# The chunk chain of a delta-rule mixer: three dependent products per chunk, or one map per chunk multiplied out ahead

## The chip, the cores and the metric

One core of one Trainium2 chip runs the whole kernel. The metric is the device time of one execution in microseconds (us). Before the change it was 1698.63 us, the median of three runs (1697.1 to 1699.03).

## The reference

One layer of a streaming encoder: a modulated RMS norm, one input projection, two groups of heads side by side (eight RWKV-7 heads with a matrix state, eight attention heads with a forget bias), an output projection, and a SwiGLU feed-forward part. 1024 frames of a new stream and 64 frames that continue an old one are handled in one launch, all in fp32 accuracy. What the change touches is the RWKV-7 recurrence, written frame by frame:

```python
def step(s, inp):
    r_t, w_t, k_t, v_t, kk_t, a_t = inp
    sa = jnp.einsum('bhvk,bhk->bhv', s, -kk_t)
    s = (s * w_t[:, :, None, :]
         + sa[..., None] * (kk_t * a_t)[:, :, None, :]
         + v_t[..., None] * k_t[:, :, None, :])
    return s, jnp.einsum('bhvk,bhk->bhv', s, r_t)
```

## The kernel before

**Stages.** The kernel first forms the modulation (`pada`), then runs a mixing stage of two halves (half 0: frames 0 to 511; half 1: frames 512 to 1023 and the 64 continued ones), in which the input projection (`pmm`, L321 to L323: three fp32r products per weight tile, with high and low parts), the RWKV heads and the preparation of attention are interleaved. Then come the attention of half 0 (`psc`, `ppt`, `pav`), the attention of half 1 with the output projection (`po`), and the feed-forward part (`pf..`, `pd`). The two strings in `ORDER` set the order in which the steps of the mixing stage are written; within that, a scheduler at build time sets the order of instructions on each engine. On the chip every engine works through its own list in order, so an instruction whose data are late holds back all that stand behind it.

**The RWKV heads.** Eight heads are four pairs j; a pair fills the 128 partitions, 64 rows per head. Step A (`rwkv_a`) makes the scaled keys and receptances (`rk`, `kb`), their score matrices `At` (`pA`, L491, per head on 64 rows), and starts the inverse of a unit triangular matrix per chunk of 64 frames. Step B (`rwkv_b`) finishes the inverse with small 32x32 products (`pg`, `pw`, `pu`, L550 to L576), transposes the keys (`pkbt`, L594) and the values (`pvt`, L602), and then walks the chunks. Half 0 has 8 chunks per pair, half 1 has 9, so 4 x 8 + 4 x 9 = 68 chunks in all. Step N normalises the outputs `y`.

**The chain over the chunks.** `sv[:, c]` is a tile of 128 partitions and two heads: for head h one half of the partitions holds the state, the other half the values of the chunk. Per chunk five products are issued, of which three depend on each other:

- `pR` (L624): scores times `sv`, the right side of the triangular system; the diagonal halves are copied to `R` by VectorE (L626) and ScalarE (L627).
- `pSA` (L637): the inverse times `R`; with a minus sign it replaces the state in `sv` (VectorE L638, ScalarE L639).
- `pS` (L640): the transposed keys times `sv`; two instructions of VectorE (L644) multiply by the decay `pc` and add `sd`, the decayed old state that GpSimd formed (L631). The result is the state in `sv` of the next chunk.
- `pY` (L635 and L645): two products that add up the outputs, one with the state, one with what replaced it.

An fp32 product of the program is two MATMUL instructions on the chip, a transpose is one. PSUM tags around the change: `rb` has one buffer (transposes, small products, `pY`, and the norm of step N), `ch` two (small products, `pR`, `pSA`, `pS`), `ra` two (`pA`).

## Time and profile before

| | |
|---|---|
| time, median of three runs | 1698.63 us |
| span of the profiled execution, first to last instruction | 1691.4 us |
| that span against the median | 7.2 us shorter: what lies around the first and the last instruction |
| mean granted TensorE clock | 0.992 |
| mixing stage, from about 60 to 664 us | 604 us |
| attention of half 0, to about 763 us | 99 us |
| attention of half 1, output projection and feed-forward part | from 763 us on |

The profile lists one execution. Its own time is not listed apart from its span; the 7.2 us are taken as fixed. Engines are PE (TensorE products), PEld (TensorE weight loads), DVE (VectorE), ACT (ScalarE), POOL (GpSimd) and SP (the queue that issues DMAs). A row of the timeline gives the start in us, the duration in us, engine, line, operation, output<-inputs, shape and count. Two rows that follow each other show what an instruction really takes from PE: products are pipelined, so the distance from start to start is shorter than the duration. A row of a group gives busy time and mean ns of one, then the engine's idle time before it. A row of waits gives total us, times, and the longest.

### The profile page before, as it was taken

To read this page: it belongs to the slowest core of one execution; us is meant where nothing else is said; L and a number is where in the kernel's file an instruction comes from. 1 tells how busy PE (TensorE), PEld (TensorE's weight loads), DVE (VectorE), ACT (ScalarE), POOL (GpSimd) and SP (SyncE) were. 2 spreads that over 40 slices of the span, in tenths; PEclk is the share of its full clock that TensorE was granted. 3 is DMA by queue.
4 is the path that set the end of the run, shared out by engine and by line. 5 is a ranking of instruction groups with operands and counts; after the bars stand their busy time and mean duration, and the time that the engine had idled before them with its cause. 6 is when DMAs were issued, how large, how long until landed. Compare 5 with 4: busy or idle time off the path is not lost.

```text
span 1691.4 us, 33224 instructions
## 1 busy us (share of the span) xinstructions
PE 1642.2 (97%) x12891; PEld 1438.5 (85%) x12891; DVE 1122.1 (66%) x2561; ACT 725.6 (43%) x1524; POOL 184.7 (11%) x412
## 2 busy tenths in 40 slices
PE   6999999999999999989999999999999999999999
PEld 3776776788888888667889899999999999999998
DVE  6776676757867655886887985555555556545545
ACT  4535364653545345775776633333333333111210
POOL 2102230222121212201220000000000000000000
PEclk9999999999999999998999999999999999999999
DMA  8544447541233344466564532222222215423313
GB/s 310 163 129 132 141 136 201 175 124 33 72 85 85 81 136 115 144 203 177 156 194 153 178 121 78 77 77 77 78 77 77 77 65 178 146 87 97 97 38 125
DMA packets 133580, 207.08 MB, mean 122 GB/s; under 512 B 62126, under 2 KB 70350, under 8 KB 133422
## 3 DMA queue, kind: packets, MB, share of 16 engines
q1 hardware_dynamic: 133422, 204.95, 39.6%
q8 instruction: 102, 1.67, 0.4%
q14 instruction: 56, 0.46, 0.1%
HBM read 157.65 MB, written 47.25 MB: 121 GB/s over the span
## 4 chain that ended last, share of the span: by engine, by line
PE 85%; ACT 5%; DVE 5%; DMA 4%; issue 2%; SPq 0%; ACTq 0%; DVEq 0%
PE pd L1302 15%; PE pfe L1187 8%; PE pfc L1187 7%; PE pfa L1187 7%; PE pmm L321 5%; PE pmm L322 5%; PE pmm L323 5%; PE pfb L1187 4%; PE pbs L402 2%; PE pav L989 2%; PE ppt L967 2%; PE pA L491 2%; PE po L321 2%; PE po L322 2%; PE po L323 2%
## 5 line engine op out<-in xcount | busy, mean ns | idle before, releaser
L321 PE MATMUL pmm<-hhi,whi 128*128 128x288 f32 (+1 forms) x624 | 218.2, 350 | 2.4 <-ACT pb L344 1.4
L322 PE MATMUL pmm<-hlo,whi 128*128 128x288 f32 (+1 forms) x624 | 216.4, 347 | 0.7 <-DVE hlo L299 0.7
L323 PE MATMUL pmm<-hhi,wlo 128*128 128x288 f32 (+1 forms) x624 | 214.7, 344 | 0.6 <-DVE wlo L243 0.6
L239 ACT CAST whi<-wraw 128x1024 fp32r<-128x1024 f32 (+2 forms) x116 | 99.2, 855 | 210.0 <-PE pd L1302 163.6
L1302 PE MATMUL pd<-al,whi 128*128 128x512 f32 (+1 forms) x528 | 172.4, 326 | 0.0
L1302 PE MATMUL pd<-ah,whi 128*128 128x512 f32 (+1 forms) x528 | 172.2, 326 | 0.0
L1302 PE MATMUL pd<-ah,wlo 128*128 128x512 f32 (+1 forms) x528 | 172.2, 326 | 0.0
L1306 DVE SCALAR_TENSOR_TENSOR x1t<-pd,mod,x1t 128x512 f32<-128x512 f32 x192 | 91.2, 498 | 106.6 <-PE pd L1302 105.9
L321 PEld LDWEIGHTS pmm<-hhi,whi 128*128 128x128 f32 x624 | 118.4, 190 | 13.9 <-ACT pb L344 2.0
L322 PEld LDWEIGHTS pmm<-hlo,whi 128*128 128x128 f32 x624 | 118.2, 189 | 10.9 <-DVE hlo L299 1.4
L323 PEld LDWEIGHTS pmm<-hhi,wlo 128*128 128x128 f32 x624 | 118.1, 189 | 10.7 <-issue 1.7
L243 DVE TENSOR_TENSOR wlo<-wraw,whi 128x1024 fp32r<-128x1024 f32 (+2 forms) x108 | 104.2, 964 | 19.5 <-ACT whi L239 18.7
L1302 PEld LDWEIGHTS pd<-ah,whi 128*128 128x128 f32 x528 | 99.1, 188 | 7.1
L1302 PEld LDWEIGHTS pd<-ah,wlo 128*128 128x128 f32 x528 | 99.1, 188 | 7.1
L1302 PEld LDWEIGHTS pd<-al,whi 128*128 128x128 f32 x528 | 99.1, 188 | 6.9
L1187 PE MATMUL pfc<-hh,hS 128*128 128x256 f32 (+1 forms) x352 | 101.8, 289 | 1.1 <-ACT hh L1089 1.1
L1187 PE MATMUL pfa<-hh,whi 128*128 128x256 f32 (+1 forms) x352 | 102.1, 290 | 0.0
L1187 PE MATMUL pfc<-hh,lS 128*128 128x256 f32 (+1 forms) x352 | 101.8, 289 | 0.0
L1187 PE MATMUL pfa<-hl,whi 128*128 128x256 f32 (+1 forms) x352 | 101.6, 289 | 0.0
L1187 PE MATMUL pfa<-hh,wlo 128*128 128x256 f32 (+1 forms) x352 | 101.5, 289 | 0.0
L1187 PE MATMUL pfc<-hl,hS 128*128 128x256 f32 (+1 forms) x352 | 100.7, 286 | 0.0
L631 POOL TENSOR_SCALAR sd<-sv,pc 64x64 f32<-64x64 f32 x136 | 77.0, 566 | 181.3 <-DVE sv L644 157.7
(368 smaller groups left out, 4380.7 us busy)
## 6 DMA issues: line engine op xcount, KB each, us to landing
wraw<-in_w_in_dram SPq DMA_DIRECT2D x52, 512.0 KB
wada<-in_w_ada_dram SPq DMA_DIRECT2D x48, 512.0 KB
as<-actscr SPq DMA_DIRECT2D x22, 544.0 KB
wraw<-in_w_gate_dram SPq DMA_DIRECT2D x22, 512.0 KB
wraw<-in_w_up_dram SPq DMA_DIRECT2D x22, 512.0 KB
wraw<-in_w_down_dram SPq DMA_DIRECT2D x40, 256.0 KB
wraw<-in_w_out_dram SPq DMA_DIRECT2D x16, 512.0 KB
actscr<-sg SPq DMA_DIRECT2D x22, 288.0 KB
```

Of the source, the lines that this page charges most:

```text
L239: nc.scalar.copy(hi, src)
L243: eng.tensor_tensor(lo, src, hi.bitcast(F32), op=ALU.subtract)
L321: nc.tensor.matmul(ps[0:M, 0:n], whi[:, k, 0:M], xhi[:, k, off:off + n], start=(k == 0), stop=False)
L322: nc.tensor.matmul(ps[0:M, 0:n], whi[:, k, 0:M], xlo[:, k, off:off + n], start=False, stop=False)
L323: nc.tensor.matmul(ps[0:M, 0:n], wlo[:, k, 0:M], xhi[:, k, off:off + n], start=False, stop=(k == kt - 1))
L402: nc.tensor.matmul(ps[:, 0:n], w, x[:, off:off + n], start=True, stop=True)
L491: nc.tensor.matmul(pa[h][:, i], kb[hp, c + i], rk[hp, c + i], start=True, stop=True)
L631: nc.gpsimd.tensor_scalar(sd[hsl[h]], sv[hsl[h], c, h], pc[hsl[h], c], None, op0=ALU.mult)
L967: nc.tensor.transpose(pt[0:rows, b - b0, t * P:t * P + qn], p[0:qn, pc:pc + rows], self.ident[0:qn, 0:qn])
L1187: nc.tensor.matmul(ps, l[:, k], r[:, s, k], start=(first and k == 0 and y == 0), stop=(k == 3 and y == 2), skip_group_check=True)
L1302: nc.tensor.matmul(ps[:, 0:n], w[:, i], x[:, t:t + n], start=(i == 0 and y == 0), stop=(i == len(fs) - 1 and y == 2))
L1306: nc.vector.scalar_tensor_tensor(dst, ps[:, so - off:so - off + l], self.mod[:, 40 + o, b:b + 1], dst, op0=ALU.mult, op1=ALU.add)
```

## The change

The walk over the chunks is a linear map of (state, values). The changed kernel multiplies that map out for each chunk before the walk, four chunks ("a quad") at a time. The score matrices of the chunk are transposed (`pat`) and copied to `gT`; the inverse is applied (`pgT`) and copied back to `gT`; two products per chunk, one per head on 64 rows (`pM`), give what is subtracted from the keys and the receptances, whose state blocks hold an identity and the decayed receptances. `kb` and `rk` now lie side by side in one tile `kr`, so that one subtraction per head and quad does both. In the walk one product per chunk gives the next state (`pS`, evacuated with the decay by one instruction of VectorE and one of ScalarE), and one gives the outputs (`pY`). `pR`, `pSA`, the second `pY`, `R`, `sd` and GpSimd's two instructions per chunk are gone. The transposes of keys and values are written ahead of the small products.

```diff
@@ rwkv_a
-        rk = self.rpool.tile([P, 9, P], F32, tag="rk", name="rk")
-        kb = self.rpool.tile([P, 9, P], F32, tag="kb", name="kb")
+        kr = self.rpool.tile([P, 9, 2, P], F32, tag="kr", name="kr")
+        kb, rk = kr[:, :, 0], kr[:, :, 1]
@@ rwkv_b
+        quads = [slice(c, min(nch, c + 4)) for c in range(0, nch, 4)]
...
         for h in range(2):
             nc.gpsimd.tensor_copy(At[hs, 0:nch, 0, h], rk[hs, 0:nch, 0:64])
         nc.gpsimd.tensor_copy(rk[0:64, 0:nch, 0:64], rk[0:64, 0:nch, 64:128])
-        nc.gpsimd.memset(rk[0:64, 0:nch, 64:128], 0.0)
-        nc.gpsimd.memset(rk[64:128, 0:nch, 0:64], 0.0)
+        nc.gpsimd.tensor_copy(rk[0:64, 0:nch, 64:128], At[0:64, 0:nch, 1, 1])
+        nc.gpsimd.tensor_copy(rk[64:128, 0:nch, 0:64], At[64:128, 0:nch, 1, 0])
+
+        gT = self.rpool.tile([P, 9, P], F32, tag="gT", name="gT")
+        for q in quads:
+            pt = self.ps([P, 4, P], tag="rb", name="pat")
+            for i, c in enumerate(range(q.start, q.stop)):
+                nc.tensor.transpose(pt[:, i], At[:, c, 0], self.ident)
+            nc.scalar.copy(gT[:, q], pt[:, 0:q.stop - q.start])
+        for h in range(2):
+            hs = hsl[h]
+            nc.gpsimd.tensor_copy(At[hs, 0:nch, 0, h], kb[hs, 0:nch, hs])
+            nc.gpsimd.tensor_copy(kb[hs, 0:nch, hs], self.ident[hs, hs].unsqueeze(1).to_broadcast([64, nch, 64]))
+        for q in quads:
+            m = q.stop - q.start
+            pt = self.ps([P, 4, P], tag="rb", name="pgT")
+            for i, c in enumerate(range(q.start, q.stop)):
+                nc.tensor.matmul(pt[:, i], inv[:, c], gT[:, c], start=True, stop=True)
+            nc.scalar.copy(gT[:, q], pt[:, 0:m])
+            pm = [self.ps([P, 4, 2, 64], tag="ch", name="pM") for _ in range(2)]
+            for i, c in enumerate(range(q.start, q.stop)):
                 for h in range(2):
+                    nc.tensor.matmul(pm[h][:, i], gT[hsl[h], c], At[hsl[h], c, :, h], start=True, stop=True)
+            for h in range(2):
+                nc.vector.tensor_tensor(kr[:, q, :, hsl[h]], kr[:, q, :, hsl[h]], pm[h][:, 0:m], op=ALU.subtract)
...
-            pr = self.ps([P, 2, 64], tag="ch", name="pR")
-            nc.tensor.matmul(pr, At[:, c, 0], sv[:, c], start=True, stop=True)
...
-            nc.tensor.matmul(pa, inv[:, c], R, start=True, stop=True)
...
-            nc.tensor.matmul(pS, kbt[:, c], sv[:, c], start=True, stop=True)
...
+                ps = self.ps([P, 2, 64], tag="ch", name="pS")
+                nc.tensor.matmul(ps, kb[:, c], sv[:, c], start=True, stop=True)
+                last = c == 7 or c == nch - 1
+                s0, s1 = (S[hsl[0]], S[hsl[1]]) if last else (sv[hsl[0], c + 1, 0], sv[hsl[1], c + 1, 1])
+                nc.vector.tensor_scalar(s0, ps[hsl[0], 0], pc[hsl[0], c], None, op0=ALU.mult)
+                nc.scalar.activation(s1, ps[hsl[1], 1], AF.Copy, scale=pc[hsl[1], c])
+            py = self.ps([P, 4, 2, 64], tag="rb", name="pY")
+            for i, c in enumerate(range(q.start, q.stop)):
+                nc.tensor.matmul(py[:, i], sv[:, c], rk[:, c], start=True, stop=True)
@@ run
-            self.rpool = MP("r", (("inv0", 1), ("inv1", 1), ("pc", 2), ("rk", 2), ("kb", 2), ("At", 2), ("gt", 1), ("g1", 1),
-                                  ("sv", 2), ("R", 2), ("st", 1), ("sd", 2)))
+            self.rpool = MP("r", (("inv0", 1), ("inv1", 1), ("pc", 2), ("kr", 2), ("At", 2), ("gt", 1), ("g1", 1),
+                                  ("sv", 2), ("gT", 1), ("st", 1)))
```

What the scheduler makes of it on PE is shown at three places; numbers L.. are lines of each kernel's own file, and a row is a product of the program (two MATMULs for fp32). First, on PE, one chunk in a walk of half 1, before:

```order
L624 MATMUL pR<-sv,At 128x128
L635 MATMUL pY<-rk,sv 128x128
L323 MATMUL pmm<-hhi,wlo 128x288
L321 MATMUL pmm<-hhi,whi 128x288
L322 MATMUL pmm<-hlo,whi 128x288
L637 MATMUL pSA<-R,inv_693 128x64
L323 MATMUL pmm<-hhi,wlo 128x288
L321 MATMUL pmm<-hhi,whi 128x288
L322 MATMUL pmm<-hlo,whi 128x288
L323 MATMUL pmm<-hhi,wlo 128x288
L321 MATMUL pmm<-hhi,whi 128x288
L640 MATMUL pS<-sv,kb 128x128
```

and one chunk there after the change:

```order
L646 MATMUL pS<-sv,kr 128x128
L653 MATMUL pY<-kr,sv 128x128
L323 MATMUL pmm<-hhi,wlo 128x288
L321 MATMUL pmm<-hhi,whi 128x288
L322 MATMUL pmm<-hlo,whi 128x288
L323 MATMUL pmm<-hhi,wlo 128x288
L646 MATMUL pS<-sv,kr 128x128
L653 MATMUL pY<-kr,sv 128x128
```

Three places at which PE has to wait for an evacuation (`pR`, `pSA`, `pS`), with 3 to 6 projection products between them, became one (`pS`), with 4 to 6 between one `pS` and the next.

Second, on PE, the multiplying out for two quads of the same pair after the change (nothing stands for it before; x8 are four chunks times two heads, the heads alternating):

```order
L323 MATMUL pmm<-hhi,wlo 128x288
L628 MATMUL pM<-At,gT 128x128 x8
L623 MATMUL pgT<-gT,inv_687 128x128 x4
L321 MATMUL pmm<-hhi,whi 128x288
L322 MATMUL pmm<-hlo,whi 128x288
L323 MATMUL pmm<-hhi,wlo 128x288
L321 MATMUL pmm<-hhi,whi 128x288
L322 MATMUL pmm<-hlo,whi 128x288
L323 MATMUL pmm<-hhi,wlo 128x288
L628 MATMUL pM<-At,gT 128x128 x8
L623 MATMUL pgT<-gT,inv_687 128x128
```

Projection products stand between a product and the one that needs its copy; `pgT` of the next quad directly follows `pM` of this one.

Third, on PE, the last pair's walk in half 1 before, which stands among the products of the attention of half 0 (`psc`, `ppt`, `pav`) from its first chunk on:

```order
L624 MATMUL pR<-sv,At 128x128
L939 MATMUL psc<-k2x_8033,q2x_8031 128x512
L602 MATMUL pvt<-ident,z 64x128
L943 LDWEIGHTS identb
L943 MATMUL psc<-cmask,identb 128x128
L635 MATMUL pY<-rk,sv 128x128
L637 MATMUL pSA<-R,inv_693 128x64
L989 MATMUL pav<-pth,vsx_8029 128x256
L640 MATMUL pS<-sv,kb 128x128
L645 MATMUL pY<-At,sv 128x128
L967 MATMUL ppt<-ident,p 128x128 x3
L989 MATMUL pav<-ptl,vsx_8029 128x256
```

and after, where the first product of attention comes after the walk's fifth `pS`, the first row here:

```order
L646 MATMUL pS<-sv,kr 128x128
L653 MATMUL pY<-kr,sv 128x128
L846 MATMUL pkv<-ident,fv 128x128
L942 MATMUL psc<-k1x_7653,qsx_7651 128x256
L944 MATMUL psc<-k2x_7654,q2x_7652 128x256
L948 LDWEIGHTS identb
L948 MATMUL psc<-cmask,identb 128x128
L646 MATMUL pS<-sv,kr 128x128
L653 MATMUL pY<-kr,sv 128x128
```

The last pair's small products, its multiplying out and five of its nine chunks now stand ahead of the attention, among the projection's products; four chunks stay in it.

## The prediction

> **What bounds the kernel now.** I read the page first, then the busy time by stage, then the stage of the change row by row.

> ```profile
> span 1691.4 us, 33224 instructions
> PE 1642.2 (97%) x12891; PEld 1438.5 (85%) x12891; DVE 1122.1 (66%) x2561; ACT 725.6 (43%) x1524; POOL 184.7 (11%) x412
> PE 85%; ACT 5%; DVE 5%; DMA 4%; issue 2%; SPq 0%; ACTq 0%; DVEq 0%
> ```

> The span is 1691.4 us and the median 1698.63, so 7.2 us lie around the span; they stay. PE is busy 97% of the span and makes 85% of the chain that ended last. So a stage gets shorter by what PE has to do less, or wait less, in it. The windows of the two stages in which the heads' walks run (core, then busy time and count of PE, PEld, DVE, ACT, POOL, the granted clock, DMA):

> ```profile
> 60.00:664.00 604.00, 589.87 (x5278) 473.11 (x5278) 418.47 (x1141) 295.06 (x660) 128.98 (x262) 1.00 0.41 116
> 664.00:763.00 99.00, 87.79 (x641) 67.25 (x634) 77.98 (x232) 70.39 (x204) 19.20 (x61) 0.97 0.58 172
> ```

> In the mixing stage PE idles 14 of 604 us, and no other engine is above 70%. In the attention of half 0 PE idles 11 of 99 us and DVE is at 79%. Seven of the eight walks lie in the first, the last one in the second.

> **What a chunk costs PE now.** Durations overlap, so I count from start to start. These are all the groups of PE in one walk of nine chunks, from its first `pR` to its end:

> ```profile
> L323 PE MATMUL pmm<-hhi,wlo 128*128 128x288 f32 x45 | 14.3, 319 | 0.0
> L321 PE MATMUL pmm<-hhi,whi 128*128 128x288 f32 x44 | 14.0, 319 | 0.0
> L322 PE MATMUL pmm<-hlo,whi 128*128 128x288 f32 x44 | 13.5, 308 | 0.0
> L624 PE MATMUL pR<-sv,At 128*128 128x128 f32 x18 | 3.9, 299 | 0.3 <-ACT sv L605 0.2
> L637 PE MATMUL pSA<-R,inv 128*128 128x64 f32 x18 | 3.7, 290 | 0.3 <-ACT R L627 0.2
> L640 PE MATMUL pS<-sv,kb 128*128 128x128 f32 x16 | 3.7, 311 | 0.1
> L635 PE MATMUL pY<-rk,sv 128*128 128x128 f32 x18 | 3.5, 279 | 0.3 <-issue 0.3
> L645 PE MATMUL pY<-At,sv 128*128 128x128 f32 x16 | 3.1, 275 | 0.0
> L402 PE MATMUL pbs<-fsq,bones 128*128 128x288 f32 x6 | 2.1, 432 | 0.0
> L602 PE MATMUL pvt<-ident,z 128*64 128x128 f32 x1 | 0.3, 292 | 0.0
> ```

> The stretch runs from 613.8 to 648.5 us, 34.7 us (two records of `pS` and of the second `pY` are missing). What a product takes when nothing waits is read from the timeline:

> ```profile
> 575.51 0.39 PE L645 MATMUL pY<-At,sv 128*128 128x128 f32 x2
> 575.74 0.39 PE L624 MATMUL pR<-sv,At 128*128 128x128 f32 x2
> 575.88 0.38 PE L322 MATMUL pmm<-hlo,whi 128*128 128x288 f32 x1
> 576.09 0.29 PE L323 MATMUL pmm<-hhi,wlo 128*128 128x288 f32 x1
> ...
> 576.49 0.29 PE L323 MATMUL pmm<-hhi,wlo 128*128 128x288 f32 x1
> ```

> A projection product takes 0.133 us (576.09 to 576.49, three steps with two rows between). An fp32 product of 128 columns takes 0.23 (575.51 to 575.74); followed by a projection product it takes 0.14, but that one then takes 0.21, so 0.22 in all. I take 0.225. The 133 projection products take 17.7 us; take away 2.1 and 0.3 for `pbs` and `pvt` (at their busy time, the upper bound), and 14.6 us are left for nine chunks: **1.62 us per chunk**. Of these the four full products are 0.9 and `pSA` with 64 columns, between half of one and one, about 0.2: 1.1 us of work. The other 0.5 us are waits, and the waits of the weight loads say the same (total us, times, longest):

> ```profile
> PEld pS L640 <- ACT sv L639: 14.1, 37, 1.2
> PEld pSA L637 <- ACT R L627: 10.9, 39, 0.6
> PEld pR L624 <- issue: 7.9, 27, 0.4
> PEld pkbt L594 <- ACT kb L595: 1.3, 5, 0.4
> ```

> 14.1, 10.9 and 7.9 are 32.9 us, 0.48 for each of 68 chunks.

> **What a chunk costs PE afterwards: the walk.** `pS` and one `pY` are 0.45 us. One wait stays. Its length is seen at today's `pSA`, which is evacuated as the new `pS` will be, one instruction of DVE and one of ACT into `sv`:

> ```profile
> 562.90 0.43 PE L637 MATMUL pSA<-R,inv 128*128 128x64 f32 x2
> ...
> 564.03 0.49 PE L640 MATMUL pS<-sv,kb 128*128 128x128 f32 x2
> ...
> L638 DVE TENSOR_SCALAR sv<-pSA 64x64 f32<-64x64 f32 x68 | 14.6, 215 | 26.6 <-PE pSA L637 22.9 <-PE pY L635 2.8 <-PE psc L943 0.4
> L639 ACT ACTIVATE sv<-pSA 64x64 f32<-64x64 f32 x68 | 14.9, 219 | 31.3 <-DVE sv L638 26.3 <-DVE z L359 1.5 <-DVE lq L754 1.0
> ```

> From product to dependent product 1.13 us. The order after the change has `pS`, `pY` and four to six projection products from one `pS` to the next, 0.45 + 4 to 6 x 0.133 = 0.98 to 1.25 us of work. So the wait is between 0 and some 0.5 (if DVE or ACT are late with other work); I take today's mean of that wait, 14.1/68 = 0.2. Walk: **0.65 us**.

> [...]

> **The multiplying out**, per quad of four chunks:

> ```profile
> 145.91 0.60 PE L594 MATMUL pkbt<-ident,kb 128*128 128x128 f32 x4
> 146.34 0.27 PE L199 MATMUL pada<-ident,mrow 128*128 128x128 f32 x1
> ...
> 595.26 0.29 PE L322 MATMUL pmm<-hlo,whi 128*128 128x288 f32 x1
> 595.48 1.17 PE L491 MATMUL pA<-rk,kb 64*128 64x128 f32 x16
> 596.57 0.75 PE L395 MATMUL plora<-z,wg 128*128 128x288 f32 x2
> ...
> 597.50 1.67 PE L491 MATMUL pA<-rk,kb 64*128 64x128 f32 x16
> 599.10 0.28 PE L550 MATMUL pg<-gt,At 32*32 32x32 f32 x6
> ```

> - `pat`: four transposes, as `pkbt`: 0.43 us.
> - `pgT`: four fp32 products, 4 x 0.225 plus the 0.08 that the next product loses: 0.98 us.
> - `pM`: eight products on 64 rows, of `pA`'s shape. `pA` took 1.09 us for eight where the heads alternate (595.48 to 596.57), 1.60 where they mostly do not. In the new order `pM` alternates throughout, so 1.09, plus the 0.09 by which the row ahead of it is longer (0.22 in place of 0.133): 1.18 us. The bound on the other side is 1.7.
> - Three hand-overs (ACT copies `pat`, ACT copies `pgT`, DVE subtracts `pM`), each with projection products placed across it. Today's of that kind cost 1.3 us in 5 waits over 20 groups of `pkbt`; I take 0.1 each, 0.3 us, though the new chain is tighter; nothing at all is one bound, the price without cover is in the rivals.

> Sum 2.9 us, **0.72 us per chunk**, and 1.37 with the walk: 0.25 less than now, 68 x 0.25 = 17 us. The ninth chunk of half 1 is multiplied out alone: 0.11 + 0.3 + 0.4 + 0.3 = 1.1 in place of 0.72, four times, 1.5 us back. That leaves **-15.5 us**.

> **The other engines.**

> ```profile
> L644 DVE SCALAR_TENSOR_TENSOR sv<-pS,pc,sd 64x64 f32<-64x64 f32 x112 | 31.6, 282 | 17.3 <-PE pS L640 14.3
> L493 DVE TENSOR_TENSOR At<-pA,amask 128x512 f32<-128x512 f32 x32 | 21.4, 686 | 8.9 <-PE pA L491 8.5
> L595 ACT COPY kb<-pkbt 128x512 f32<-128x512 f32 x16 | 9.4, 588 | 10.1 <-PE pkbt L594 10.0
> L631 POOL TENSOR_SCALAR sd<-sv,pc 64x64 f32<-64x64 f32 x136 | 77.0, 566 | 181.3 <-DVE sv L644 157.7 <-DVE tb L515 8.7 <-DVE state L644 5.2
> L583 POOL COPY rk<-rk 64x576 f32<-64x576 f32 x4 | 2.7, 672 | 0.2
> ```

> DVE loses per chunk a copy of about 0.215, one scaling of 0.215 and two instructions of 0.282, and gains a scaling of 0.215 and half of a subtraction like L493, 0.686 x 2 / 4: 0.99 becomes 0.56 us. ACT loses two instructions of about 0.21, gains one and two copies of 0.588 per quad: 0.43 becomes 0.51 us. POOL loses 77 us of `sd` and gets four more copies of about 0.65 per walk. Neither sets the pace of the mixing stage, so I cost these at nothing there. POOL's copies stand between the transposes of `At` and `pM`; they take 2.6 us, and `pat`, `pgT` and their two copies take about that, with projection products besides. Without that cover they would cost up to 2.6 x 8 = 21 us. No queue of DMAs is moved.

> In the attention of half 0, DVE is at 79%, and nine chunks put 9 x 0.99 = 9 us on it. In the new order five of the nine stand ahead of the attention and the others are cheaper. If DVE sets the pace there, that is up to 9/0.79, some 10 us; if hand-overs between engines do, nothing, and the work only moves. I take 2. **-17.5 us: 1681 us.**

> **The rivals.**

> *The hand-overs are not covered* (slower). `pat`, copy, `pgT`, copy, `pM` and subtraction follow each other through one `rb` buffer and two `ch` buffers, and PE goes through its list in order. A bare hand-over costs 0.35 us of a product's own latency (0.49 long, 0.14 to the next start) and its evacuation: 0.94 for each copy, 1.7 for two subtractions, 3.6 us per quad, 58 us for 16 full quads and about 6 for the four single chunks. I have charged 6, so uncovered it would be 58 more, 1739. The sign turns when a group waits 0.9 us longer than I charged. Half covered it gives 1710. For it: a buffer fewer than needed, and engines that are late with other work. Against it: three to six projection products, 0.4 to 0.8 us, stand at each hand-over in the order, and today's `pkbt` waited 1.3 us in all.

> *The one wait takes the place of three* (no change). If evacuations come late because DVE and ACT have the new copies and subtractions ahead of them, `pS` waits 0.45 in place of 0.2: 17 us back, 1698. For it: `pS` to `pS` has 0.98 to 1.25 us of work across 1.13 us. Against it: DVE gets a third less to do than it loses on PE's path.

> *The attention gains what I halved away* (faster still). All of the 10 us in place of 2, and waits of 0.1 at `pS`: -32 us, 1667. For it: DVE at 79% there, the walk's DVE work nearly gone from it. Against it: the work that moves ahead is PE's in a stage where PE is full.

> *The change does not do what it says*: PE's list has more products than before (11053 against 10985), but the order shows the dependent ones gone, so I give this no chance of its own.

> **How the numbers follow.** Forecast 0.60, 1681; more from the attention 0.16, 1667; the wait that stays 0.12, 1698; uncovered hand-overs 0.12, 1710. The forecast's own range is 1673 to 1690 (`pM` at 1.7, hand-overs at nothing or 0.2, attention at 0 to 5). The range of 1664 to 1699 takes in the second and third case and leaves out the slower one. 0.2%, 3.4 us, is about what a measurement of this kernel can tell from no change; faster than 1695.2 are the first two and a little of the third, 0.78; within, 0.09; slower, 0.13.

> **What would show it.** In the profile after: in a walk of half 1, its stretch less 0.133 per projection product gives 0.65 us per chunk; the weight loads of `pS` wait some 14 us in all and those of `pat`, `pgT` and `pM` under 10; eight `pM` take 1.1 us; DVE's subtractions take 0.69 each; the stage from the last projection product to the first `po` is a few us shorter. The prediction is wrong if PE's waits for `gT` or `kr` reach 20 us, or if the mixing stage is as long as before with PE as full.

## The result: 1.6% slower, at a lower clock

The changed kernel takes 1726.37 us (median of four executions, 1716.08 to 1727.34) against 1697.87 us before in the same comparison: 28.5 us slower, a ratio of 1.0163 with a 95% interval of 1.0134 to 1.0193. The forecast was 1681. Two executions of the kernel before, of 2223 and 3087 us where all others lie between 1691 and 1701, were in a slower state and are left out of every figure.

The page of the changed kernel, its profiled execution (1727.34 us):

```profile
span 1725.6 us, 32896 instructions
PE 1660.7 (96%) x12959; PEld 1456.4 (84%) x12959; DVE 1105.6 (64%) x2397; ACT 733.0 (42%) x1496; POOL 137.5 (8%) x308
PEclk9999998999897999998999999999999999999999
PE 83%; DVE 6%; ACT 5%; DMA 3%; issue 1%; POOL 1%; SPq 0%; DVEq 0%; ACTq 0%
```

PE still bounds the kernel, and its busy share is nearly the same. What differs is its clock: 0.971 on average against 0.992. The granted clock is under 0.9 in four of the 40 slices; before it was in one:

```profile
PEclk9999999999999999998999999999999999999999
```

The windows of the mixing stage, of the attention of half 0, and of four stretches of the mixing stage (columns as in the prediction; the number behind POOL's is the granted clock):

```profile
60.00:705.00 645.00, 627.66 (x5585) 507.52 (x5584) 415.63 (x1016) 311.56 (x662) 91.70 (x178) 0.94 0.40 113
705.00:772.00 67.00, 54.28 (x313) 38.73 (x311) 54.58 (x167) 49.51 (x149) 8.91 (x39) 1.00 0.56 174
250.00:300.00 50.00, 47.51 (x405) 33.77 (x406) 29.68 (x81) 22.80 (x47) 4.76 (x7) 0.84 0.70 213
500.00:550.00 50.00, 44.88 (x400) 36.96 (x399) 31.27 (x66) 25.74 (x55) 4.01 (x8) 0.86 0.30 74
550.00:600.00 50.00, 49.96 (x370) 44.29 (x370) 30.66 (x68) 22.43 (x49) 9.72 (x18) 0.87 0.32 77
600.00:650.00 50.00, 49.31 (x553) 42.01 (x552) 32.47 (x92) 20.12 (x50) 5.96 (x9) 1.00 0.44 130
```

The mixing stage became 40 us longer (its last projection product ends at 705 us in place of 665), though PE idles in it 17 us in place of 14: PE is *busy* 37 us longer. From 550 to 600 us it is busy all the time and gets through 370 products; from 600 to 650, at the full clock, through 553. Such a count also hangs on how large the products are; before, at the full clock, the same two stretches had 471 and 393:

```profile
550.00:600.00 50.00, 49.45 (x471) 42.18 (x471) 35.37 (x93) 18.72 (x47) 11.97 (x25) 1.00 0.35 100
600.00:650.00 50.00, 48.23 (x393) 41.68 (x393) 24.30 (x87) 23.76 (x65) 11.82 (x22) 1.00 0.43 109
```

What the clock costs is seen better in single products, on PE's timeline around 540 us:

```profile
538.14 0.30 PE L321 MATMUL pmm<-hhi,whi 128*128 128x288 f32 x1
538.27 0.30 PE L322 MATMUL pmm<-hlo,whi 128*128 128x288 f32 x1
...
540.20 0.29 PE L323 MATMUL pmm<-hhi,wlo 128*128 128x288 f32 x1
542.38 0.30 PE L559 MATMUL pvt<-ident,z 128*64 128x128 f32 x1 [1.89 <-ACT sv L562]
542.81 0.52 PE L321 MATMUL pmm<-hhi,whi 128*128 128x288 f32 x1
543.13 0.44 PE L322 MATMUL pmm<-hlo,whi 128*128 128x288 f32 x1
543.38 0.44 PE L323 MATMUL pmm<-hhi,wlo 128*128 128x288 f32 x1
...
553.09 0.44 PE L322 MATMUL pmm<-hlo,whi 128*128 128x288 f32 x1
553.33 0.44 PE L323 MATMUL pmm<-hhi,wlo 128*128 128x288 f32 x1
```

`pvt`, one of the transposes that the change moved ahead of the small products, waits 1.89 us for ScalarE (`rb` has one buffer, and the copies of the `pvt` before it are late), and the projection product behind it on PE's list starts only after it, at 542.81 us. From 542.9 us on a projection product takes 0.24 us from start to start in place of 0.133, and it still does so ten microseconds later, with PE busy throughout. The trace lists the granted clock. In this execution it is either 1.00 or 0.50, and the time from one change to the next is a whole number of times 3.41 us throughout: the stretch at 0.50 that begins here lasts from 542.9 to 563.4 us, six times 3.41. In the span there are twelve stretches at 0.50, of 3.4 to 20.5 us, 99 us in all; before there were five, of 3.4 to 10.2 us, 27 us in all. The mixing stage has 0.94 on average, which is 75 of 645 us at 0.50 ("at the half clock" from here on); before it was 3 us. What goes ahead of such stretches is taken up at e13 to e17.

### The profile page after: what moved, and what is told of

Same layout as the page of the kernel before. It is cut to its first block, busy times and chain, and to the rows that moved or that the text cites. A ratio compares the mean times of both kernels' runs of the same rounds, so it can differ in the third digit from the quotient of the medians.

```text
span 1725.6 us, 32896 instructions
## 1 busy us (share of the span) xinstructions
PE 1660.7 (96%) x12959; PEld 1456.4 (84%) x12959; DVE 1105.6 (64%) x2397; ACT 733.0 (42%) x1496; POOL 137.5 (8%) x308
## 3 DMA queue, kind: packets, MB, share of 16 engines
q8 instruction: 102, 1.67, 0.4%
## 4 chain that ended last, share of the span: by engine, by line
PE 83%; DVE 6%; ACT 5%; DMA 3%; issue 1%; POOL 1%; SPq 0%; DVEq 0%; ACTq 0%
PE pd L1307 15%; PE pfe L1192 7%; PE pfc L1192 7%; PE pfa L1192 7%; PE pmm L321 5%; PE pmm L323 5%; PE pmm L322 5%; PE pfb L1192 4%; PE pav L994 2%; PE pbs L402 2%; PE pA L491 2%; PE ppt L972 2%; PE po L321 2%; PE po L322 2%; PE po L323 2%
## 5 line engine op out<-in xcount | busy, mean ns | idle before, releaser
L321 PE MATMUL pmm<-hhi,whi 128*128 128x288 f32 (+1 forms) x624 | 224.7, 361 | 3.9 <-ACT pb L344 3.8
L323 PE MATMUL pmm<-hhi,wlo 128*128 128x288 f32 (+1 forms) x624 | 219.4, 352 | 0.6 <-DVE wlo L243 0.6
L322 PE MATMUL pmm<-hlo,whi 128*128 128x288 f32 (+1 forms) x624 | 219.0, 351 | 0.7 <-DVE hlo L299 0.6
L321 PEld LDWEIGHTS pmm<-hhi,whi 128*128 128x128 f32 x624 | 123.0, 197 | 19.6 <-ACT pb L344 5.6
L323 PEld LDWEIGHTS pmm<-hhi,wlo 128*128 128x128 f32 x624 | 123.0, 197 | 12.9 <-issue 1.6
L322 PEld LDWEIGHTS pmm<-hlo,whi 128*128 128x128 f32 x624 | 123.6, 198 | 11.4 <-DVE hlo L299 1.5
L1139 ACT CAST hS<-wraw 128x512 fp32r<-128x512 f32 x88 | 53.6, 620 | 62.4 <-PE pfc L1192 61.5
```

The costliest lines, as they stand in the source:

```text
L321: nc.tensor.matmul(ps[0:M, 0:n], whi[:, k, 0:M], xhi[:, k, off:off + n], start=(k == 0), stop=False)
L322: nc.tensor.matmul(ps[0:M, 0:n], whi[:, k, 0:M], xlo[:, k, off:off + n], start=False, stop=False)
L323: nc.tensor.matmul(ps[0:M, 0:n], wlo[:, k, 0:M], xhi[:, k, off:off + n], start=False, stop=(k == kt - 1))
L1139: nc.scalar.copy(w[x][0], src)
```

## The experiments

Each run lists its span and its mean granted clock. With two levels, the time at the half clock is 2 x (1 - mean clock) x span; for the changed kernel 2 x 0.029 x 1725.6 = 100 us. Ten executions of one kernel (e6 below), the same instructions in the same order each time, show what that is worth (us, mean clock):

```
1700.19 0.987   1700.38 0.986   1702.15 0.985   1709.69 0.980   1711.34 0.979
1711.42 0.979   1715.18 0.976   1717.97 0.973   1719.53 0.972   1720.56 0.971
```

The time follows the clock, over 20 us, in one and the same program. Fitted within each kernel over the 141 executions of this study, **1 us at the half clock costs 0.37 us**. A dense product loses 0.45 of its time there (0.24 in place of 0.133), and time in which PE waits for others should, by my estimate, lose less, so a price somewhat under 0.45 fits the clock as the cause; only one execution of each kernel has a trace, so what else differs between executions is not seen. The last column of the table takes 0.37 us off the mean time (1724.0 for the changed kernel) for each us at the half clock: what the kernel would need at the full clock. It is an estimate, good to some 1 us.

| kernel | median us (executions) | ratio to before, 95% | us at half clock, mean | full clock, us |
|---|---|---|---|---|
| before | 1695.4 (49) | | 24 (10 to 34) | 1686.9 |
| changed | 1726.4 (4) | 1.0163, 1.0134 to 1.0193 | 96 (72 to 110) | 1688.6 |
| e1_back | 1708.1 (6) | 1.0079, 1.0053 to 1.0104 | 55 | 1687.6 |
| e2_ahead | 1725.4 (4) | 1.0176, 1.0156 to 1.0197 | 73 | 1698.6 |
| e3_fill | 1736.7 (4) | 1.0249, 1.0225 to 1.0273 | 47 | 1720.6 |
| e4_fill_before | 1751.3 (4) | 1.0331, 1.0301 to 1.0362 | 62 | 1729.0 |
| e5_state | 1712.2 (4) | 1.0095, 1.0071 to 1.0118 | 60 | 1690.5 |
| e6_ra | 1711.4 (10) | 1.0085, 1.0055 to 1.0115 | 73 (44 to 100) | 1684.2 |
| e7_quad_ra | 1735.4 (4) | 1.0246, 1.0210 to 1.0282 | 100 | 1699.9 |
| e8_late | 1718.4 (4) | 1.0133, 1.0108 to 1.0157 | 84 | 1688.0 |
| e9_masks | 1713.8 (4) | 1.0102, 1.0084 to 1.0120 | 67 | 1688.7 |
| e10_ra_masks | 1711.6 (4) | 1.0111, 1.0066 to 1.0156 | 77 | 1686.5 |
| e11_swap_before | 1694.4 (10) | 0.9996, 0.9983 to 1.0009 | 23 (17 to 34) | 1686.3 |
| e12_swap_after | 1713.0 (4) | 1.0114, 1.0072 to 1.0157 | 73 (58 to 100) | 1688.6 |
| e13_marks | 1705.5 (4) | 1.0061, 1.0043 to 1.0079 | 28 | 1695.2 |
| e14_short_waits | 1710.7 (4) | 1.0096, 1.0075 to 1.0118 | 26 | 1702.0 |
| e15_long_waits | 1704.9 (4) | 1.0058, 1.0042 to 1.0074 | 26 | 1695.3 |
| e16_small_products | 1748.7 (4) | 1.0317, 1.0301 to 1.0333 | 73 | 1722.2 |
| e17_longer_waits | 1703.7 (6) | 1.0053, 1.0037 to 1.0069 | 26 | 1694.8 |
| e18_split | 1792.7 (4) | 1.0562, 1.0536 to 1.0589 | 172 | 1728.6 |

Of the 28.5 us, (96 - 24) x 0.37 = **27 us are the clock**. The other 2 are a second miss: at the full clock the change was to save 17.5 us and saves none.

### Which part of the change: e1 and e2

e1 puts the transposes of keys and values back behind the small products, in the changed kernel:

```diff
-        for q in quads:
-            pt = self.ps([P, 4, P], tag="rb", name="pkbt")
...
         for h, (r0, r1) in enumerate(rr):
             nc.scalar.copy(inv[r0, 0:nch, r1], pg[h][r0, 0:nch])
...
+        for q in quads:
+            pt = self.ps([P, 4, P], tag="rb", name="pkbt")
...
```

> The changed kernel, with the transposes of the keys and the values written behind the small 32x32 products again, where the kernel before had them. Theory A (the loss is time that PE spends at the half clock in the mixing stage, and the gaps that begin it come from the transposes standing ahead of the small products): the stretches at the half clock fall from some 99 us to under 50, the granted clock rises to 0.985 or more, and the time is 1690 to 1700. Theory B (the half clock comes from the small products themselves, once the walks no longer fill in between): the half-clock time stays near 90 us and the time at 1720 to 1730. Theory C (the hand-overs of the multiplying out cost the time): 1720 to 1730, with the clock as it may be, and with waits of pat, pgT and pM that account for the 28 us.

e2 moves the same block ahead of the small products, in the kernel before.

> The kernel before, with one part of the change alone: the transposes of the keys and the values are written ahead of the small products. Theory A (this part begins the half-clock stretches): half-clock time rises from some 27 us to 60 or more, and the time to 1715 to 1730. Theories B and C: no such rise, 1695 to 1702.

The windows of the mixing stage, of e1 and then of e2:

```profile
60.00:682.00 622.00, 604.88 (x5581) 487.63 (x5580) 417.91 (x1015) 311.68 (x661) 92.45 (x178) 0.98 0.41 117
```

```profile
60.00:695.00 635.00, 613.64 (x5451) 492.78 (x5450) 424.22 (x1154) 299.93 (x680) 132.97 (x269) 0.97 0.40 113
```

The moved transposes alone make the kernel before 30 us slower, as theory A had it: 18 by the clock (49 us more at half) and 12 at the full clock, of which PE's idle time in the mixing stage shows 7 (21 us against 14). Undoing that part of the change gives 18 of its 28 us back. That is less than theory A asked for: e1 has 55 us at half and 1708.1 us, where A had under 50 and 1690 to 1700. So the place of the transposes is the larger part of the loss, not all of it; what is left in e1 is clock too, 55 us at half against 24.

### Dense products between the small ones: e3 and e4

`fill` is called behind each of the five groups of small products; `last` is the group's last product:

```diff
+        def fill(last):
+            with self.tc.issue_after(last.ins):
+                pf = self.ps([P, 512], tag="ra", name="pfill")
+                for _ in range(3):
+                    nc.tensor.matmul(pf, self.whi2[0][:, 0:P], self.hhi[:, 0, 0:512], start=True, stop=True)
...
+            fill(last)
```

> The changed kernel, with three added dense products (128x512, fp32r) behind each group of small products of the inverse; what they make isn't used. They are 120 products of about 0.234 us, 28 us of added PE work. If time at the half clock is the loss (A and B alike): the clock in the mixing stage returns to about 0.99 to 1.00, which gives back up to 36 us, so that the time is 1715 to 1728 in spite of the added work, and less the 28 us it is below 1700. If hand-overs are the loss (C): the added work comes on top in full or in good part, 1740 to 1755.

> The kernel before, with the same added products, so that their own price is seen where the clock is nearly whole: 28 us of work on an engine that is 98% busy in this stage, 1718 to 1728. Less than 1715 would say that the added products stand in gaps.

e3 raised the clock as expected of the half-clock theories (96 to 47 us at half; 0.99 in the mixing stage), but its 28 us of added products cost 32 at the full clock, so it is 10 us slower than the changed kernel, between the two expectations. e4 missed: 56 us slower, of which 42 at the full clock and 14 by the clock. The added products don't stand in gaps. They are 28 us of work; where the other 14 at the full clock come from was not tried (PE idles 8 us more in the mixing stage than before).

### The start of the kernel: e5 and e9

In the changed kernel PE stands still for 3 us at the start, and a stretch at the half clock follows (51.4 to 54.8 us). Rows of GpSimd, ScalarE and PE from its timeline:

```profile
41.08 0.21 POOL L119 MEMSET bones<- 128x128 f32 x1 [18.68 <-DVE hlo L299]
...
46.47 0.24 ACT L634 COPY sv<-state 64x64 f32<-64x64 f32 x1 [3.69 <-POOL state L164]
...
51.30 0.72 PE L321 MATMUL pmm<-hhi,whi 128*128 128x512 f32 x1 [2.95 <-ACT pb L344]
```

GpSimd's memsets of masks wait for VectorE's last `hlo` (before the change they ran at 22 us), and the memsets of `wlo` and `state` come behind them, 4.5 us later than before (`state` at 46.28 us in place of 41.77). That the new pools put `bones` where earlier data still lay is likely, but was not tried. e5 is e1 with the states' memsets written ahead of the masks:

```diff
+        self.state = [f.tile([P, 64], F32, name=f"state{j}") for j in range(4)]
+        for t in self.state:
+            nc.gpsimd.memset(t, 0.0)
         self.bones = f.tile([P, P], F32, name="bones")
```

e9 is e1 with the memsets of all masks written behind that of `cmul`, which stands last:

```diff
-        for t, v in ((self.bones, 1.0), (self.bmean, 1.0 / 64)):
-            nc.gpsimd.memset(t, 0.0)
...
         nc.gpsimd.memset(self.cmul.rearrange("p (c t) -> p c t", t=64)[:, :, 0:1], 0.0)
+        for t, v in ((self.bones, 1.0), (self.bmean, 1.0 / 64)):
+            nc.gpsimd.memset(t, 0.0)
...
```

> The kernel of e1_back, with GpSimd's memsets of the initial states written ahead of those of the masks. In the changed kernel and in e1_back these come 4.4 us later than before, ScalarE waits 3.7 us for one, and PE waits 3 us behind that, with a stretch at the half clock at 51 us. Theory D (this wait costs what it lasts and the half clock after it): the wait and that stretch are gone, and the time is 4 to 6 us under e1_back's 1708, 1702 to 1704. Theory S (any new order shifts the time by what half-clock stretches it happens to bring): the wait goes, but the time is anywhere from 1698 to 1715, as the clock goes.

> The kernel of e1_back, with GpSimd's memsets of the masks (bones, bmean, tri, amask) written behind those of wlo, the states and cmul, so that both wlo and the states come as early as before. In e5_state the states came early, but wlo did not, VectorE waited 2.4 us for it, and PE's wait of 3 us at 50 us stayed. Theory D (that wait is some 4 us of the loss, by itself and by the half clock behind it): PE's wait and the half-clock stretch at 52 us are gone, and the time that is left after taking 0.37 us for each us at the half clock off (1687.7 for e1_back, 1687.0 before) falls by 3 to 4 us to 1684; the time itself to 1695 to 1705, as the clock goes. Otherwise it stays at 1687 to 1691.

In e5 ScalarE's wait went, but VectorE waited 2.3 us for `wlo` and PE's wait stayed (2.7 us); the time, 1712, lies where theory S had it. In e9 PE's wait and the stretch at 52 us went; yet the time at the full clock stayed at 1688.7 (e1: 1687.6). Theory D's price is not confirmed: what was saved at 50 us was lost by 94 (the 157th projection product starts at 94.5 us, in e1 at 84.3), 4.5 us of it in waits for `pb`, where e1 has 0.8.

### Buffers: e6, e7 and e10

In e6, on the changed kernel, this is the edit for `pkbt` and `pvt`; e10 is e6 with e9's edit of the masks; e7 is e5 with the same edit for `pat` and `pgT`:

```diff
-            pt = self.ps([P, 4, P], tag="rb", name="pkbt")
+            pt = self.ps([P, 4, P], tag="ra", name="pkbt")
```

> The changed kernel as it is, transposes of the keys and values ahead of the small products, but with their outputs in the PSUM tag ra (two buffers) in place of rb (one buffer). Theory B1 (it is the queue for the one rb buffer that makes PE wait and lets the clock fall): waits of pvt and pkbt fall from some 9 us to under 4, the half-clock time in the mixing stage from 81 us to under 45, the time to 1700 to 1712. Theory B2 (it is the place: with the transposes out of the way nothing dense stands between the small products and the multiplying out, whichever buffer they use): half-clock time stays over 60 us and the time at 1718 or more.

> The kernel of e5_state with the outputs of pat and pgT in the tag ra in place of rb, so that the multiplying out no longer shares one buffer with the outputs pY and the norm. If hand-overs of the multiplying out still hold PE (theory C): 5 to 15 us under e5_state. If they do not (the prediction's 0.1 us for each): within 4 us of e5_state, unless the clock goes the other way.

> The same edit of the masks on the kernel of e6_ra. If both edits add up: 1684.3 less 3 to 4 us, some 1681 at the full clock, and 1700 to 1710 as measured if it keeps e6_ra's 73 us at the half clock; under 1695 if the new order brings no more than 40 us. If they don't add up: 1684 and over at the full clock.

e6's profiled execution is as theory B1 had it: the weight loads of `pvt` and `pkbt` wait 2.5 us (5.7 in the changed kernel), the mixing stage has 44 us at the half clock (75), and the time is 1711. The way is less clear. From start to start the transposes take more of PE, 20 us in place of 15, and over ten executions the time at the half clock runs from 44 to 100 us, 73 on average; so how much the one `rb` buffer is to blame is not settled. e6 has the best time at the full clock of the kernels with the new chain, 1684.2. e7 is 23 us over e5, which neither branch of its expectation had: with `pat` and `pgT` in `ra`, beside `pA`, `plora` and `pbs`, the multiplying out took 59 us of PE in place of 46. e10's two edits did not add up (1686.5 at the full clock, over e6's 1684.2).

### The attention: e8

PE's timeline of the changed kernel has two waits at the first heads of half 1 that the kernel before has not:

```profile
778.52 1.19 PE L942 MATMUL psc<-k1x,qsx 128*128 128x512 f32 x2 [3.46 <-DMA k1x<-kx]
781.77 0.79 PE L944 MATMUL psc<-k2x,q2x 68*128 68x512 f32 x1 [2.06 <-DMA k2x<-kx]
```

e8 is e5 with the last pair's step B written later:

```diff
-... P B3 K2 k3 k2 V3
+... P K2 k3 B3 k2 V3
```

> The kernel of e5_state with the last pair's step B written two steps later in half 1 (P K2 k3 B3 k2 V3), so that all nine chunks of its walk stand in the attention of half 0 again, as before the change. Theory E (the attention of half 1 waits 6 to 7 us for its operands because the shorter half 0 leaves their transfers no cover): the wait of psc for k1x and k2x falls under 2 us and the time is 5 to 8 us under e5_state. Otherwise: the wait stays, and the time is within 4 us of e5_state or above.

The waits stayed (3.90 and 1.30 us), and the time rose, by 6 us over e5. In the changed kernel the queue issued these transfers from 771.57 us on, 7 us ahead of the product; why so late, and what would cover them, stays open.

### Is it chance? e11 and e12

```diff
-V0 V1 B2 V2
+V0 B2 V1 V2
```

> The kernel before, with two neighbouring steps of half 1 exchanged in ORDER (V0 B2 V1 in place of V0 V1 B2); the work is the same. Theory S (how long PE runs at the half clock hangs on the order by chance, and the kernel before has an order with little of it): half-clock time rises to 40 us or more from 25 and the time to 1700 to 1712, at an unchanged 1685 to 1689 for the full clock. Theory M (it is what the change does that brings the half clock): half-clock time stays at 20 to 35 us and the time at 1693 to 1699.

> The changed kernel with the same two steps exchanged. Theory S: its half-clock time of 96 us moves by 20 us or more, down as likely as up, and the time by 7 us or more from 1726. Theory M: 85 to 105 us at the half clock and 1721 to 1731.

A reordering of the same work leaves the kernel before where it was, in time and clock, as theory M had it. The changed one moved from 96 to 73 us at half, which is theory S's outcome: stretches do come and go with the order, though the executions of the two overlap (72 to 110, 58 to 100). But none of the eleven kernels with the new chain has under 40 us in any execution, and e11 and the kernel before have none over 34. One exchange in each is a small sample; with these numbers it speaks for the change, not for a lucky order before.

### What lowers the clock: e13 to e17

These put known waits and products into the last stage (`pd`) of the kernel before, where PE is dense and the clock full (busy for 256 of the 258 us from 1432 to 1690 us, at 1.00). This is e15; e13 has no copies, e14 one and e17 seventeen, and e13 and e14 have `o % 2 == 1`. e16 has no copies and 100 products of `stl[0:32, 0:32]`.

```diff
                         ps = self.ps([P, 512], tag="abce"[(3 * o + (t > 0) + (t > 512)) % 4], name="pd")
+                        if t == 0 and g < len(groups) - 1 and o % 8 == 1:
+                            nc.scalar.copy(self.stl, self.prev[:, 0:64])
+                            for _ in range(9):
+                                nc.scalar.copy(self.stl, self.stl)
+                            nc.tensor.matmul(ps[0:64, 0:64], self.stl, self.stl, start=True, stop=True)
+                        self.prev = ps
```

> The kernel before, with one extra product of 64x64 (two MATMULs, its result is overwritten) at 20 places of the last stage, waiting for nothing: the control for the next three. All theories: within 4 us of before.

> The same, but at each of the 20 places the extra product reads what ScalarE has just copied from the product before it, so that PE waits for one hand-over, some 0.6 to 0.9 us, 12 to 18 us in all. Theory W (a wait costs its own length as long as it is short, and lowers the clock only when it takes a good third of a 3.4 us stretch): no half-clock time in this stage, 12 to 18 us slower than e13. Theory V (any wait of PE in a dense stage lowers the clock): 20 more stretches of 3.4 us, another 20 x 3.4 x 0.45 = 31 us on top.

> The same at 5 places only, with ten copies behind one another, so that PE waits some 2.2 to 2.9 us at each, 11 to 15 us in all. Theory W: each wait is followed by 3.4 us or more at the half clock, 17 us or more in all, which costs 6 to 8 us on top of the waits: 17 to 23 us slower than e13. If long waits bring no half clock: 11 to 15 us slower.

> As e15_long_waits, but with seventeen copies behind one another, so that PE should be idle some 3.0 to 3.5 us at each of the 5 places, 15 to 17 us in all. Theory W, with the point where it decides put between 40% and 50% of a 3.4 us stretch: at least 4 of the 5 waits are followed by a half-clock stretch of 3.4 us or more, 14 to 34 us in all, which costs 5 to 12 us beside the waits; some 10 us of waits more than e15, so 1719 to 1729. If idle time doesn't lower the clock in a dense stage: none, and 1713 to 1717.

> The kernel before with 100 products of 32x32 (200 MATMULs of some 25 ns, 5 us) at the same 5 places, waiting for nothing; their results are overwritten. Theory P (a stretch filled with small products counts for the clock as if PE were idle, though its rows show it busy): the half clock follows each place, 17 us or more in all, and the time is 25 us of products and 6 to 8 us more over e13's. Theory Q (only idle time counts): 25 us, with no half-clock time in this stage.

What PE waited for in that stage, in e14 (weight loads; 20 waits), and in e15 (weight loads, then PE):

```profile
PEld pd L1305 <- ACT stl L1302: 6.7, 20, 1.5
```

```profile
PEld pd L1305 <- ACT stl L1304: 7.3, 5, 2.0
...
PE pd L1305 <- ACT stl L1304: 5.2, 4, 1.6
```

The marks alone cost 10 us for 20 (e13, expected within 4). Over that, e14's waits of 6.7 us cost 5.2, and e15's 7.3 us (with 5 marks, 2.5 us) cost 7: about their own length, and no half clock followed (the stage has 1.00 on average in e13, e14 and e15). All three kernels came out faster than any branch of their expectations, because the waits are shorter than planned. PE still had products ahead of the marked one while the copies ran, 4 to 17 of them in e15 and 15 to 28 in e17, and it never idled over 1.6 us. So single waits up to 1.6 us in an otherwise dense stage didn't lower the clock; theory V is refuted for them, and theory W, which needs longer ones, was not tried.

e16's stretch with small products and what follows it (windows):

```profile
1438.50:1441.90 3.40, 3.40 (x113) 3.40 (x110) 2.44 (x4) 0.97 (x2) 0.00 (x0) 1.00 1.00 353
1441.90:1448.70 6.80, 6.80 (x86) 6.16 (x84) 1.29 (x1) 1.10 (x1) 0.00 (x0) 0.50 1.05 402
1448.70:1452.10 3.40, 3.40 (x23) 3.14 (x22) 0.98 (x2) 1.10 (x1) 0.00 (x0) 1.00 0.39 154
```

PE is busy for every moment, waits for nothing, and the clock halves. It did so at each of the five places, 2.6 to 5.7 us after the first small product, for 6.8 to 10.2 us, 41 us in all: theory P. The transfers are not the cause: in the 3.4 us ahead of the fall the DMA engines were 100% busy at the first place but 23% at the fifth, and in e13 they were 97% busy from 1428 to 1445 us at the full clock. The time is a miss: 43 us over e13, where 31 to 33 were expected. A small MATMUL took 32 ns at the full clock in place of 25 (in the kernel before, groups of them take 14 to 33 ns each from start to start), and 53 at the half clock, and the half clock lasted 41 us, where the 6 to 8 us stand for 17. So at these five places the half clock followed 32x32 products and not idle time: PE was busy for 311.00 of the 311.00 us from 1432 to 1743 us.

With this the mixing stages can be read. I cut each, from 60 us to its last projection product, into stretches of 3.41 us, laid so that the changes of the clock in its trace fall on their ends, and call one *low* when PE idles over 30% of it or is busy with other than small products for less than half of it (the wait at 50 us, one more in the kernels with the new chain, lies ahead of this):

| kernel | low stretches in the mixing stage | of them mostly small products | us at the half clock there |
|---|---|---|---|
| before; e11 | 6; 6 | 6; 5 | 3; 7 |
| changed; e12 | 14; 14 | 10; 9 | 75; 44 |
| e1; e2 | 14; 15 | 10; 11 | 20; 37 |
| e3 | 12 | 7 | 14 |
| e18 | 35 | 15 | 113 |

Over fifteen such traces, an idle stretch at the full clock was followed by the half clock 37 times in 69, one of small products 31 in 121, any other 13 in 2406. So the count tells the kernel before from the changed one and from e18, but it does not order the kernels with 12 to 15: most low stretches are not followed by the half clock. The same traces say more when graded by the share of a full-clock stretch that PE spends on other than small products (transposes among them). Under 0.3, the half clock followed 33 times in 40; from 0.3 to 0.5, 30 times in 116; above, 18 times in 2440.

### Undoing the bunching: e18

Step `b` is the DMAs and the small products of a pair, `B` what follows them; `ORDER` reads `Q0 b0 V0 A1 C0 b1 B0 N0` at its first place, and so on:

```diff
+            elif op == "b":
+                g[j] = self.rwkv_bs(hf, j, st.pop(j))
+                next(g[j])
             elif op == "B":
-                y[j] = self.rwkv_b(hf, j, st.pop(j))
+                y[j] = finish(g.pop(j)) if j in g else self.rwkv_b(hf, j, st.pop(j))
```

> The kernel of e1_back with step B cut in two, the small products of a pair (b) and what follows them (B), and with b of the next pair written just ahead of B of the pair before. If this undoes the bunching: 15 windows of 3.4 us with PE idle or on small products for half their time become 6 to 9, as before the change, half-clock time falls from 55 to under 35 us, and the time to 1690 to 1699. If the scheduler keeps the small products together whatever the order of the steps: 10 or more such windows, 45 us or more at the half clock, 1703 or more.

It went the other way, 35 low stretches and 172 us at half, 97 us slower than before. PE idles 49 us in the mixing stage in place of 17, 6.1 of them in small products (`pg`) that wait for their data, the rest spread over many waits. The remedy failed, so whether the bunching is the cause is not tested by it; it does show more low stretches together with more half clock. No kernel of this study beats the one before.

## Why the prediction was wrong

**The step that failed** is the one under "What a chunk costs PE now": "A projection product takes 0.133 us", "I take 0.225". These durations, read at the full clock, were carried over to the changed kernel as if fixed. The mean clock stood in its table and in its windows (1.00 and 0.97), but no term, rival or bound of the sum had the clock in it. What the runs showed in its place: 96 us at the half clock against 24, where a projection product takes 0.24 us, and so 27 of the 28.5 us. The moved transposes, to which e1 and e2 trace the larger part of it, had no term either. Its last condition for being wrong came true: a longer mixing stage with PE as full. The 7.2 us that it takes as lying around the span are another slip, on which nothing in the sum hangs: an execution takes 1.7 us more than its own span (1727.34 and 1725.6), and the rest is one execution's span set against a median of three.

**The terms on the chain were right.** The groups of PE in a walk of nine chunks, 639.7 to 650.1 us (two `pM` that began before it left out), then a `pY` of this walk behind it and PE's multiplying out:

```profile
L646 PE MATMUL pS<-sv,kr 128*128 128x128 f32 x18 | 4.1, 308 | 0.3 <-ACT sv L650 0.3
L322 PE MATMUL pmm<-hlo,whi 128*128 128x288 f32 x11 | 3.6, 329 | 0.0
L323 PE MATMUL pmm<-hhi,wlo 128*128 128x288 f32 x11 | 3.5, 318 | 0.0
L321 PE MATMUL pmm<-hhi,whi 128*128 128x288 f32 x10 | 3.2, 319 | 0.0
L653 PE MATMUL pY<-kr,sv 128*128 128x128 f32 x14 | 2.7, 275 | 0.0
L402 PE MATMUL pbs<-fsq,bones 128*128 128x288 f32 x4 | 1.4, 431 | 0.0
```

```profile
652.15 0.49 PE L653 MATMUL pY<-kr,sv 128*128 128x128 f32 x2
```

```profile
632.23 1.16 PE L628 MATMUL pM<-At,gT 64*128 64x128 f32 x16
633.33 1.16 PE L623 MATMUL pgT<-gT,inv 128*128 128x128 f32 x8
634.24 0.38 PE L323 MATMUL pmm<-hhi,wlo 128*128 128x288 f32 x1
```

10.4 us less 32 x 0.133 and 1.4 is 4.7 us. Only seven of the nine `pY` stand in the stretch (14 MATMULs; the other two are at 638.0 and 652.15), so 0.45 comes on top: 5.2 us, 0.58 per chunk. With the four `pbs` at 0.9 from start to start, in place of 1.4 busy, it is 0.63 (0.65 forecast). Eight `pM` took 1.10 us (1.18), four `pgT` 0.91 (0.98).

```profile
PEld pS L646 <- ACT sv L650: 8.3, 31, 0.6
PEld pM L628 <- ACT gT L624: 2.2, 7, 0.6
PEld pM L628 <- POOL kr L618: 2.0, 4, 1.2
PEld pgT L623 <- ACT gT L614: 1.8, 5, 0.8
PEld pM L628 <- DVE kr L630: 1.2, 6, 0.2
PEld pat L613 <- ACT gT L614: 0.9, 3, 0.5
```

`pS` waited 8.3 us (14 forecast), the three hand-overs 8.1 in all (under 10). VectorE's subtractions took 0.68 us (0.69). Of the rivals, uncovered hand-overs, the only one that ended slower, is refuted by these rows, and so is one wait that takes the place of three.

**Where the gain at the full clock went.** PE's time from start to start by groups, from the first projection product to the feed-forward part, in us (in brackets what of it fell into the half clock; profiled executions):

| | before | changed | e1_back |
|---|---|---|---|
| chain: `pR pSA pS pY`, or `pat pgT pM pS pY` | 80.7 | 80.9 (7.6) | 77.0 (0.3) |
| projection products, with waits behind them | 373.9 (3.1) | 378.3 (38.0) | 376.8 (21.5) |
| small products | 50.2 (0.4) | 57.8 (16.3) | 50.1 (1.3) |
| transposes `pkbt`, `pvt` | 11.3 (1.5) | 15.0 (0.8) | 10.9 (0.7) |
| attention and `po` | 265.5 (15.6) | 272.7 (13.7) | 273.0 (13.7) |
| the rest | 136.3 | 145.8 (18.5) | 140.5 (2.7) |
| all | 918.0 (20.6) | 950.5 (94.9) | 928.3 (40.2) |

The products of the chain are nearly as much work as before, mainly the waits went: at 0.45 off for the bracketed part (an estimate), projection products fell by 11 us and the chain by 3, near the 15.5 that the prediction worked out. It was given back in places for which the prediction had no term: the moved transposes (+4), the rest, with the start in it (+1), and the attention with its output projection (+8), where the prediction took -2 (its bound there, 9/0.79, is 11 us and not 10). The stretch from the last projection product to the feed-forward part did get 7 us shorter, as part of the last walk had moved out of it, but 5.5 us of waits for transfers came in. The step "No queue of DMAs is moved" gave these waits no term. Whether they come from the shorter stage ahead is not shown: e8 put the last pair's walk back into that stage, and they stayed.

**What stays open.** Why e1, with the transposes in place, has 14 low stretches and not 6. That e1's small products have fewer projection products among them because the multiplying out uses these as cover fits the shorter walk (45 projection products of each kind in a walk of nine chunks before, 10 or 11 now), but was not tried. Nor was it shown why executions of one kernel differ in clock (0.987 to 0.971 in e6).

## What to carry to other kernels

Where PE bounds a stage, its clock is a term of the sum: count, in stretches of 3.41 us, those in which PE idles or does little but tiny products, before and after the change, and don't price them at nothing: in these traces the half clock followed 33 of 40 stretches with less than 30% of other work, and 30 of 116 with 30 to 50%. This change took 14 us off the projection products and the chain at the full clock (an estimate, from the table above), and 27 us were lost by the clock. Look also at what a change writes elsewhere "for free": here the block that was only moved cost 18 of the 28 us.
